# The end of a state-space layer: output projections of the last two groups, summed in one accumulation or apart

## The chip, the cores and the metric

One core of a Trainium2 chip runs the whole program in one launch. The metric is the device time of one execution in microseconds, as the median of three runs. The engines are TensorE (PE, with its weight loads listed as PEld), VectorE (DVE), ScalarE (ACT), GpSimd (POOL) and SyncE (SP), which issues nearly all DMAs.

## The reference, cut to what matters

The model is a trunk of two layers of three sub-layers each: an FFN, a mixer, an FFN, every one with a scaled residual and a layer norm behind it. The mixer of the first layer is a bidirectional Mamba-2 (state-space) block, that of the second a differential attention. The change touches the end of the state-space block. There are 512 positions, 1024 model channels, and an inner width of 2048 in four groups of 512.

```python
y = y_f + y_b + X * d_skip.astype(f32)[:, None]
y = y.reshape(b, t, D_INNER) * jax.nn.silu(z.astype(f32))
yg = y.reshape(b, t, SSM_GROUPS, D_INNER // SSM_GROUPS)
yg = yg * lax.rsqrt(jnp.mean(jnp.square(yg), axis=-1, keepdims=True) + LN_EPS)
y = yg.reshape(b, t, D_INNER) * norm_g.astype(f32)
return y.astype(u.dtype) @ w_out
...
x = layer_norm(ALPHA * x + gate(1) * y, ln_g[i, 1], ln_b[i, 1])
y = swiglu(modulate(x, mods[:, 2]), ffn_w_gate[i, 1], ffn_w_up[i, 1], ffn_w_down[i, 1])
```

Each group has its own RMS norm (the "gated norm"), so the output projection of a group can start when that group's scan and norm are done. The four groups' contributions to `y @ w_out` are summed.

## The kernel before, in words

Activations are kept transposed: channels on the 128 partitions, positions along the free dimension. The residual `x` is eight blocks of 128 channels by 512 positions (`res[0]` to `res[7]`). Every float32 operand of a projection is split into a high and a low part (`split` for weights, lines 107 to 125, one pass of ScalarE and one of DVE; `split_act` for activations), and a product is three matmuls: high by high, high by low, low by high (`mm3`, line 172). All projections are recorded at line 176. One output block of one group has four blocks of 128 in its inner dimension, hence 12 matmuls over 512 positions, or twice 12 over 256 positions where it is done in halves. The sum goes into a PSUM tile (`acc`; 4 banks of that tag, 2 of "mid", 2 of "ln"). `add_res` (line 400, recorded at L401) multiplies it by the gate and adds it to the residual on DVE.

`ssm` (line 651) works group by group. A scan of a group has eight steps (four pairs of heads by two halves of the sequence). Each step makes decay matrices: a DMA of broadcast rows (`rw`, `ch`), masks on POOL (L840), exponentials on ScalarE (L848 to L851), a sum on POOL (L854), a product with `cb` on DVE (L855), and then 12 matmuls on PE (L865). Between the steps the code puts "units" of other work, from a list `todo`: convolution projections of the next group, the `z` projections of this group, and output projections (`outp`, two output blocks a call, 24 matmuls) of the group before. After the projections of a group come its SiLUs in one batch (L775, with a change of ScalarE's function table before and after), and `prepare` builds the next group's matrices. Before the change the units of a scan are these, in written order:

- group 1: ten projections, then the four output units of group 0
- group 2: ten projections, then the four output units of group 1
- group 3: four `z` projections, then two of the four output units of group 2; the other two stand behind the last gated norm

`gated_norm` (line 867) multiplies by SiLU(z) (L870), sums squares (L872 to L876), makes four columns of statistics with matmuls (L879), takes the power -1/2 on POOL (L258), and in `rest` broadcasts the result with transposes (L264) and normalizes (L888, L153, L154). For groups 0 to 2 it is issued inside the scan of the next group; for group 3 nothing of a scan is left.

The layer norm behind the block subtracts a provisional mean first, the mean over the first residual block's channels (`LN.shift`, line 293: a copy at L297, a matmul at L298, a copy at L300, and four subtractions over pairs of blocks at L303). Before the change it is issued with the first output unit of group 2.

The last group's output runs through `down_units` (line 418) with KEEP 6: blocks 0 and 1 over all positions, blocks 2 to 7 kept for `finish` (line 436), which does them first for positions 0 to 255, then for 256 to 511. After each block `feed` updates the sums for the norm (L311 to L317). After each half come the statistics (`stats`: L323, L327, L332 to L341, L345) and a generator that normalizes this half (`normalize`: L368, L373, L375) while the next half's blocks are multiplied. The next FFN's first products work on the first half while the second is still being normalized; its first block over all positions stands in a "mid" bank. Beside it runs `ada_stream`, which computes the next layer's modulation from weights (DMA `in_adaw`, DVE L195).

The attention layer ends in another way, with `merged_units` (line 456). It takes two sets of four inner blocks, `old` (ready early) and `new` (ready late). Output blocks 0 to 3 are done for `old` and for `new` apart. For blocks 4 to 7 the products of both sets go into one accumulation of 24 matmuls per half; of blocks 4 and 5 the `old` products of the first half are begun early, in the "mid" banks. It is a generator: each `next` issues one block, so the caller can put blocks between other steps, and `shut` and `gated` (lines 164 to 170) tell the planner to order a matmul of the norm behind the last projection issued so far.

The code is written for a tile framework: it allocates buffers from pools with a fixed number of slots, sets all semaphores, and plans the order of each engine's instructions from its own model of time, with the written order as the priority. So the order run can differ from the order written. The pool `ap` has 32 tiles of 128 by 512 (`big`): inputs, states, normalized groups and the first weights of the next FFN live there. Weights arrive in four `raw` tiles and are split into a ring of three (`wp`). The tiles of the scan (`ep`: `rw`, `ch`, `dx`, `E` with five slots) are open until the end of the layer.

Of the kernel before, what the change touches and what calls it, by code (L numbers as in the profile page):

```python
# [14 lines left out]
P = 128  # L15
# [7 lines left out]
NG = 4  # L23
# [23 lines left out]
def hybrid_trunk(tc, xT, cb, par, cst, adaw, wgu, wdn0, wdn1, wdn2, wdt, win, wso, wqk, wv, wao, dist_in, dtp, lam_in, out):  # L47
    nc = tc.nc
# [13 lines left out]
    def big(dt=F32, name="big"):  # L62
        return ap.tile([P, T], dt, tag="a", name=name)
# [4 lines left out]
    def acc(tag="acc"):  # L68
        return ps.tile([P, T], F32, tag=tag, name=tag, bufs=BANKS[tag])
# [10 lines left out]
    invg = cp.tile([P, 1], F32, name="invg")  # L80
# [81 lines left out]
    last_mm, gate = [None], [None]  # L162

    def gated(x):
        if gate[0] is not None:
            tc.add_manual_dep(x.ins, gate[0].ins.name, NOSYNC, reason="behind a projection")
        return x

    def shut():
        gate[0] = last_mm[0]  # L170
# [11 lines left out]
    def proj(o, w, u, m=P, cols=FULL, prev=None):  # L182
        for a, b in cols:
            prev = mm3(
                o[:m, a:b], [(w[k][0], w[k][1], u[k][0][:, a:b], u[k][1][:, a:b]) for k in range(len(u))], prev
            )
        last_mm[0] = prev
        return prev
# [59 lines left out]
    def advance(g, n):  # L248
        for _ in range(n):
            if g is None or next(g, "end") == "end":  # L250
                return
# [148 lines left out]
    def add_res(d, pd, n, a, b):  # L400
        nc.vector.scalar_tensor_tensor(  # L401
            out=res[d][:, a:b], in0=pd[:, a:b], scalar=gvec[n][:, d : d + 1], in1=res[d][:, a:b],
            op0=ALU.mult, op1=ALU.add,
        )
# [13 lines left out]
    def down_units(n, u, units, ln=None, KEEP=4):  # L418

        last = ln is not None  # L420
        keep = []
        for ld in units:
            for d, w in ld():
                if last and d >= KT - KEEP:
                    keep.append((d, w))
                    continue
                pd = acc()
                proj(pd, w, u)
                add_res(d, pd, n, 0, T)
                if last:  # L430
                    ln.feed(d, 0, T)
            yield
        if last:
            finish(n, ln, [(d, w, u) for d, w in keep])
# [18 lines left out]
        next_u[0] = ln.u  # L453
        ln.residual()

    def merged_units(n, ln, old, wo, wn, home):

        half = len(old)
        for q in range(2):
            w = split(load(wo[q]))  # L460
            for e in range(2):
                pd, d = acc(), 2 * q + e
                proj(pd, w[e * 4 : e * 4 + 4], old)
                add_res(d, pd, n, 0, T)
                if d == 0:
                    shifting = ln.shift()
                advance(shifting, 1)
                yield
        w0 = {2: split(load(wo[2]), home=home[0])}
        begun = {}  # L470
        for e in range(2):
            pd = acc("mid")
            proj(pd, w0[2][e * 4 : e * 4 + 4], old, cols=HALVES[:1])
            begun[4 + e] = (pd, half)
            yield
        new = yield
        for q in range(2):
            w = split(load(wn[q]))
            for e in range(2):
                pd, d = acc(), 2 * q + e  # L480
                proj(pd, w[e * 4 : e * 4 + 4], new)
                add_res(d, pd, n, 0, T)
                ln.feed(d, 0, T)
        keep = []
        for q in range(2, 4):
            w1 = split(load(wn[q]), home=home[q - 1])
            if q == 3:
                w0[3] = split(load(wo[3]), home=home[3])
            for e in range(2):
                c = slice(e * 4, e * 4 + 4)  # L490
                keep.append((2 * q + e, w0[q][c] + w1[c], old + new))
        finish(n, ln, keep, begun)

    def send(g, x):
        try:
            g.send(x)
        except StopIteration:
            pass
# [140 lines left out]
    def wide_units(w):  # L639
        def mk(q):  # L640
            def ld():
                s = split(load(w[q]))
                return [(q * 2 + e, s[e * 4 : e * 4 + 4]) for e in range(2)]
            return ld
        return [mk(q) for q in range(4)]
# [5 lines left out]
    def ssm(n):  # L651
        u = next_u[0]
        sc = ExitStack()
        ep = sc.enter_context(tc.tile_pool(name="ep", bufs=2))
        dp = sc.enter_context(tc.tile_pool(name="dp", bufs=1, space=bass.MemoryType.DRAM))
        masks = big(name="masks")
        nc.sync.dma_start(masks, cst[:, 2 * P :])
# [206 lines left out]
                    rhs = mats[hh][:, k * W : (k + 1) * W] if k < 2 else chs[hh][:, cc]  # L864
                    nc.tensor.matmul(py[hh * 64 : (hh + 1) * 64, cc], lhsT=lhs, rhs=rhs, start=k == 0, stop=k == 2)  # L865

        def gated_norm(g, ys, zs):
            ss = big(name="gss")
            for k in range(4):
                nc.vector.tensor_tensor(out=ys[k], in0=ys[k], in1=zs[k], op=ALU.mult)  # L870
                if k == 0:
                    nc.scalar.activation(ss, ys[k], AF.Square)  # L872
                else:
                    sq = tmp("sq")
                    nc.scalar.activation(sq, ys[k], AF.Square)
                    nc.vector.tensor_tensor(out=ss, in0=ss, in1=sq, op=ALU.add)  # L876
            st = acc("ln")
            for i in range(4):
                nc.tensor.matmul(st[:, i : i + 1], lhsT=ss[:, i * P : (i + 1) * P], rhs=invg, start=True, stop=True)  # L879
            r = rstd(st[:, :4], 4)  # L880

            def rest():
                rb = acc("ln")
                bcast_cols(rb, r[:, :4])
                yr = []
                for k in range(4):
                    o = tmp("yn")
                    nc.vector.scalar_tensor_tensor(  # L888
                        out=o, in0=ys[k], scalar=pc(C_NG + g * 4 + k), in1=rb, op0=ALU.mult, op1=ALU.mult
                    )  # L890
                    yr.append(split_act(o))
                return yr

            return rest

        def run(units):
            for f in units:
                f()
# [3 lines left out]
        bc, xs, zs = [], [], [[] for _ in range(NG)]  # L902
# [6 lines left out]
        run(units_z(0, zs[0])[:2])  # L909
        cur = prepare(0, xs, bc)  # L910
        outs, yrs = {}, {}
        ln, shifting = LN(n), []
        norm = None

        def outp(gg):
            if gg not in outs:
                outs[gg] = down_units(n, yrs[gg], wide_units(wso[gg]))
                if gg == NG - 2:
                    shifting.append(ln.shift())
            next(outs[gg])  # L920
            if shifting:
                advance(shifting[0], 2)

        for g in range(NG):
            xt, cbs, states, Ct = cur
            nbc, nxs = [], []
            first = units_z(g, zs[g])[len(zs[g]) :]
            if g < NG - 1:
                first = units_bc(g + 1, nbc) + units_x(g + 1, nxs) + first
            todo = first + ([lambda gg=g - 1: outp(gg)] * 4 if g > 0 else [])  # L930
            tot, done, batched = len(todo), 0, False
            for s in range(8):
                pr_, c = divmod(s, 2)
                ft = g * 4 + pr_
                if c == 0:
                    heads = [ssd_head(ft * 2 + hh, Ct) for hh in range(2)]
                    py = acc("mid")
                mats = [ssd_mats(ft * 2 + hh, c, heads[hh][0], heads[hh][2], cbs) for hh in range(2)]
                ssd_out(pr_, c, py, mats, [hd[1] for hd in heads], xt, states)
                if c == 1:  # L940
                    nc.vector.scalar_tensor_tensor(
                        out=xs[pr_], in0=xs[pr_], scalar=pc(C_D + ft), in1=py, op0=ALU.mult, op1=ALU.add
                    )
                if s == 0 and norm is not None:
                    rest = norm()
                if s == 2 and norm is not None:
                    yrs[g - 1] = rest()
                while done < tot - (2 if g == NG - 1 else 0) and done < (s + 1) * tot // 8:
                    todo[done]()
                    done += 1  # L950
                if done >= len(first) and not batched and (s >= 6 or done == tot):
                    batched = True
                    silu(zs[g] + nbc + nxs)
                    if g < NG - 1:
                        cur = prepare(g + 1, nxs, nbc)
            norm = (lambda g=g, xs=xs: gated_norm(g, xs, zs[g]))
            xs = nxs
        yr = norm()()
        run(todo[done:])
        advance(shifting[0], 4)  # L960
        for _ in down_units(n, yr, wide_units(wso[NG - 1]), ln, 6):
            pass
        sc.close()


# [306 lines left out]
```

## Time and profile before

| | us |
|---|---|
| median of three runs | 2182.35 (2177.52 to 2185.12) |
| the profiled execution | 2177.95 |
| its span, first to last instruction | 2176.1 |
| PE busy | 2120.5 (97%) |
| DVE busy | 1765.4 (81%) |
| ACT busy | 1092.2 (50%) |
| POOL busy | 155.2 (7%) |

The scans take about 460 to 776 us of the span, with group 3's first matmul at 720.9 us; the last gated norm, the last output blocks and the layer norm go to about 840 us. The attention layer's end lies between about 1756 and 1834 us.

How to read the views: a wait row gives the engine that waited, who released it, then the total in us, the times and the longest. A chain row gives start, us and what ran, merged over neighbours with their count. A timeline row gives start, us, engine, line, operation, operands, count and, in brackets, the idle time before it and its releaser. Window rows give the stretch, its length, busy time of each engine with the count of its instructions, the granted share of TensorE's clock, the DMA share and GB/s. A busy PE is not PE at its peak, so the text counts matmuls and their spacing. A few per cent of the matmul records may be missing.

### The profile page before, as it was taken

The page shows a single profiled execution, that of the slowest core. Times are in us where ns is not written, and L with a number is a line of the kernel's source. Part 1 is how long each engine was busy: PE and PEld are TensorE (multiplying, and loading weights), DVE is VectorE, ACT ScalarE, POOL GpSimd, SP SyncE. Part 2 cuts the span into 40 slices and gives each one's busy share as a digit, 9 for nine tenths or more (in the row PEclk, how much of TensorE's full clock was granted, in tenths as well). Part 3 has the DMA queues.
Part 4 walks back from the last instruction along what each step waited for, and adds up shares of the span by engine and source line. Part 5 has one row for each costly group of instructions (what it writes and reads, how often), then busy time and mean ns, then how long its engine had stood idle before and what let it go on. Part 6 is the DMA issues. An engine that isn't in the chain of part 4 may idle for free.

```text
span 2176.1 us, 34041 instructions
## 1 busy us (share of the span) xinstructions
PE 2120.5 (97%) x13206; PEld 1857.6 (85%) x13206; DVE 1765.4 (81%) x2934; ACT 1092.2 (50%) x1828; POOL 155.2 (7%) x258
## 2 busy tenths in 40 slices
PE   7999999999999998999999999999999999999997
PEld 6889899866777677989899989899988878989897
DVE  6979998556666688979988998997777888958696
ACT  4424354757656546434355534344766647524353
POOL 0000000034332310000000000000111100000000
PEclk9999999999999998999999999999999999999999
DMA  8853644464445413554533272733322212423231
GB/s 320 304 213 118 222 130 166 115 181 136 145 126 158 123 64 126 174 185 153 196 125 112 95 265 92 254 100 124 89 78 78 88 44 84 136 70 116 77 117 40
DMA packets 90082, 301.19 MB, mean 138 GB/s; under 512 B 10048, under 2 KB 13504, under 8 KB 89920
## 3 DMA queue, kind: packets, MB, share of 16 engines
q1 hardware_dynamic: 88384, 294.81, 41.3%
q0 software_dynamic: 1536, 4.20, 0.9%
q8 instruction: 104, 1.70, 0.3%
q14 instruction: 58, 0.48, 0.1%
HBM read 289.53 MB, written 5.24 MB: 135 GB/s over the span
## 4 chain that ended last, share of the span: by engine, by line
PE 84%; DVE 5%; issue 4%; ACT 3%; POOL 2%; DMA 2%; POOLq 0%; SPq 0%; ACTq 0%; DVEq 0%
PE acc L176 67%; PE mid L176 10%; PE mid L865 2%; DMA raw<-in_adaw 1%; PE mid L1033 1%; DVE raw L195 1%; POOL E L854 1%; PE ln L176 1%; PE ln L813 1%; DMA raw<-in_wdn 0%; ACT wh L123 0%; ACT p L1043 0%; PE ln L1055 0%; POOL dx L840 0%; PE ln L264 0%
## 5 line engine op out<-in xcount | busy, mean ns | idle before, releaser
L176 PE MATMUL acc<-hi,wh 128*128 128x256 f32 (+1 forms) x1576 | 526.9, 336 | 3.1 <-ACT hi L153 1.9
L176 PE MATMUL acc<-hi,wl 128*128 128x256 f32 (+1 forms) x1576 | 525.9, 334 | 0.0
L176 PE MATMUL acc<-lo,wh 128*128 128x256 f32 (+1 forms) x1576 | 525.6, 334 | 0.3 <-DVE lo L154 0.2
L176 PE MATMUL acc<-uh,wh 128*128 128x256 f32 (+1 forms) x1160 | 391.8, 338 | 0.2 <-ACT wh L123 0.2
L176 PE MATMUL acc<-ul,wh 128*128 128x256 f32 (+1 forms) x1160 | 390.5, 337 | 0.0
L176 PE MATMUL acc<-uh,wl 128*128 128x256 f32 (+1 forms) x1160 | 389.5, 336 | 0.0
L123 ACT ACTIVATE wh<-raw 128x1024 fp32r<-128x1024 f32 (+1 forms) x210 | 213.0, 1022 | 272.7 <-DMA raw<-in_wdn 95.9
L528 ACT ACTIVATE wh<-raw 128x1024 fp32r<-128x1024 f32 x198 | 209.1, 1059 | 254.1 <-DVE raw L538 121.8
L176 PEld LDWEIGHTS acc<-hi,wh 128*128 128x128 f32 x1576 | 297.9, 189 | 40.1 <-ACT hi L153 5.2
L176 PEld LDWEIGHTS acc<-lo,wh 128*128 128x128 f32 x1576 | 298.0, 189 | 31.8 <-DVE lo L154 1.9
L176 PEld LDWEIGHTS acc<-hi,wl 128*128 128x128 f32 x1576 | 298.0, 189 | 29.9 <-issue 0.5
L124 DVE TENSOR_TENSOR wl<-raw,wh 128x1024 fp32r<-128x1024 f32 (+1 forms) x210 | 248.0, 1184 | 47.6 <-ACT wh L123 46.7
L529 DVE TENSOR_TENSOR wl<-raw,wh 128x1024 fp32r<-128x1024 f32 x198 | 241.2, 1220 | 24.0 <-ACT wh L528 23.0
L176 PEld LDWEIGHTS acc<-uh,wh 128*128 128x128 f32 x1160 | 219.3, 189 | 29.6 <-issue 6.6
L176 PEld LDWEIGHTS acc<-ul,wh 128*128 128x128 f32 x1160 | 219.7, 189 | 24.9 <-issue 3.3
L176 PEld LDWEIGHTS acc<-uh,wl 128*128 128x128 f32 x1160 | 219.7, 189 | 23.9 <-issue 2.4
L538 DVE TENSOR_TENSOR raw<-raw 128x512 f32<-128x512 f32 x264 | 181.3, 689 | 4.7
L195 DVE SCALAR_TENSOR_TENSOR raw<-raw,cond 128x1024 f32<-128x1024 f32 x144 | 174.1, 1221 | 9.6 <-DMA raw<-in_adaw 9.4
L401 DVE SCALAR_TENSOR_TENSOR resid<-acc,gv,resid 128x512 f32<-128x512 f32 (+1 forms) x164 | 108.6, 667 | 71.1 <-PE acc L176 70.8
L341 POOL TENSOR_TENSOR rr<-vr,mhalf 128x2 f32<-128x2 f32 x12 | 9.5, 789 | 1512.9 <-DVE vr L337 1512.9
L176 PE MATMUL mid<-uh,wh 128*128 128x256 f32 (+2 forms) x332 | 99.6, 302 | 0.6 <-DVE up L570 0.6
L176 PE MATMUL mid<-uh,wl 128*128 128x256 f32 (+2 forms) x332 | 99.3, 299 | 0.0
(267 smaller groups left out, 3939.6 us busy)
## 6 DMA issues: line engine op xcount, KB each, us to landing
raw<-in_wgu SPq DMA_DIRECT2D x176, 512.0 KB, 4.0
raw<-in_adaw SPq DMA_DIRECT2D x144, 512.0 KB, 4.7
raw<-in_wdn SPq DMA_DIRECT2D x64, 448.0 KB, 4.0
raw<-in_win SPq DMA_DIRECT2D x40, 512.0 KB, 3.8
raw<-in_wdn SPq DMA_DIRECT2D x32, 512.0 KB, 4.7
rw<-scr SPq DMA_DIRECT2D x32, 512.0 KB, 5.5
ch<-scr SPq DMA_DIRECT2D x32, 256.0 KB, 3.6
raw<-in_wso SPq DMA_DIRECT2D x16, 512.0 KB, 3.6
```

Of the source, the lines that this page charges most:

```text
L123: nc.scalar.activation(hi[:, :n], raw, AF.Copy)
L124: nc.vector.tensor_tensor(out=lo[:, :n], in0=raw, in1=hi[:, :n].bitcast(F32), op=ALU.subtract)
L176: last = nc.tensor.matmul(o, lhsT=a, rhs=b, start=start and j == 0, stop=j == n - 1, skip_group_check=not start)
L195: nc.vector.scalar_tensor_tensor(out=raw, in0=raw, scalar=1.0, in1=cond, op0=ALU.mult, op1=ALU.mult, accum_out=mods[l][:, j : j + 1],)
L401: nc.vector.scalar_tensor_tensor(out=res[d][:, a:b], in0=pd[:, a:b], scalar=gvec[n][:, d : d + 1], in1=res[d][:, a:b], op0=ALU.mult, op1=A ...
L528: nc.scalar.activation(x[0], r, AF.Copy)
L529: nc.vector.tensor_tensor(out=x[1], in0=r, in1=x[0].bitcast(F32), op=ALU.subtract)
L538: nc.vector.tensor_tensor(out=o, in0=x, in1=y, op=ALU.add)
L813: nc.tensor.matmul(pst, lhsT=bt[:, i * P : (i + 1) * P], rhs=xd, start=o == 0, stop=o == 1)
L854: nc.gpsimd.tensor_tensor(out=dg, in0=dg, in1=dx[:, c], op=ALU.add)
L865: nc.tensor.matmul(py[hh * 64 : (hh + 1) * 64, cc], lhsT=lhs, rhs=rhs, start=k == 0, stop=k == 2)
L1033: nc.tensor.matmul(ss[m], lhsT=q[:, c], rhs=qks[h, 1][m], start=j == 0, stop=j == 1)
```

## The change

The last two groups' outputs go through `merged_units`, with group 2's normalized blocks as `old` and group 3's as `new`:

- Output units move by two: of group 1's four, two stay at the end of group 2's scan and two go to the end of group 3's. None of group 2's stand inside a scan.
- The last gated norm gets a `fill`: two output blocks of group 2 are issued ahead of its statistics, and one between the power and the broadcast. The matmuls of the norm are ordered behind them. Block 3 and the begun halves of blocks 4 and 5 follow after the broadcast.
- Output blocks 4 to 7 sum groups 2 and 3 in one accumulation, in halves; blocks 0 to 3 of group 3 go over all positions.
- `shift` is created before the scans and advanced one step at a time in group 3's scan, from step 3 on.
- The pool `ep` is closed after the scans, and a weight ring `wy` of three is opened in its place for three of the late weight tiles.

For the attention layer `merged_units` does the same as before.

```diff
-    def merged_units(n, ln, old, wo, wn, home):
+    def merged_units(n, ln, old, wo, wn, home, shifting=None):
...
-                if d == 0:
-                    shifting = ln.shift()
+                shifting = shifting or ln.shift()
                 advance(shifting, 1)
...
-        def gated_norm(g, ys, zs):
+        def gated_norm(g, ys, zs, fill=None):
...
+            if fill:
+                fill(2)
             st = acc("ln")
             for i in range(4):
-                nc.tensor.matmul(st[:, i : i + 1], lhsT=ss[:, i * P : (i + 1) * P], rhs=invg, start=True, stop=True)
+                gated(nc.tensor.matmul(st[:, i : i + 1], lhsT=ss[:, i * P : (i + 1) * P], rhs=invg, start=True, stop=True))
...
             def rest():
+                if fill:
+                    fill(1)
                 rb = acc("ln")
...
-        ln, shifting = LN(n), []
+        ln = LN(n)
+        shifting = ln.shift()
...
-            todo = first + ([lambda gg=g - 1: outp(gg)] * 4 if g > 0 else [])
+            late = lambda gg, k: [lambda: outp(gg)] * k
+            todo = first + (late(0, 4) if g == 1 else late(1, 2) if g > 1 else [])
...
-                while done < tot - (2 if g == NG - 1 else 0) and done < (s + 1) * tot // 8:
+                while done < (s + 1) * tot // 8:
...
+                if g == NG - 1 and s > 2:
+                    advance(shifting, 1)
...
-        yr = norm()()
-        run(todo[done:])
-        advance(shifting[0], 4)
-        for _ in down_units(n, yr, wide_units(wso[NG - 1]), ln, 6):
-            pass
+        es.close()
+        wy = sc.enter_context(tc.tile_pool(name="wy", bufs=3))
+        tail = merged_units(n, ln, yrs[NG - 2], wso[NG - 2], wso[NG - 1], (wy, wy, None, wy), shifting)
+
+        def fill(k):
+            for _ in range(k):
+                next(tail)
+            shut()
+
+        yr = norm(fill)()
+        gate[0] = None
+        for _ in range(4):
+            next(tail)
+        send(tail, yr)
```

More of the change, by code (lines that the diff above doesn't have):

```diff
@@ L653, in ssm @@
         sc = ExitStack()
-        ep = sc.enter_context(tc.tile_pool(name="ep", bufs=2))
+        es = ExitStack()
+        ep = es.enter_context(tc.tile_pool(name="ep", bufs=2))
         dp = sc.enter_context(tc.tile_pool(name="dp", bufs=1, space=bass.MemoryType.DRAM))
@@ L917, in outp @@
                 outs[gg] = down_units(n, yrs[gg], wide_units(wso[gg]))
-                if gg == NG - 2:
-                    shifting.append(ln.shift())
             next(outs[gg])
-            if shifting:
-                advance(shifting[0], 2)
         for g in range(NG):
@@ L955, in ssm @@
                         cur = prepare(g + 1, nxs, nbc)
-            norm = (lambda g=g, xs=xs: gated_norm(g, xs, zs[g]))
+            norm = (lambda fill=None, g=g, xs=xs: gated_norm(g, xs, zs[g], fill))
             xs = nxs
-        yr = norm()()
-        run(todo[done:])
-        advance(shifting[0], 4)
-        for _ in down_units(n, yr, wide_units(wso[NG - 1]), ln, 6):
-            pass
+        es.close()
[10 more added lines that the diff above has]
+        send(tail, yr)
         sc.close()
```

## The prediction

> **What bounds the kernel now.** I read the page first, then PE's waits around the end of the state-space layer, then windows and the chain there, and last the same views of the attention end, which already runs the `merged_units` tail.
>
> ```profile
> span 2176.1 us, 34041 instructions
> PE 84%; DVE 5%; issue 4%; ACT 3%; POOL 2%; DMA 2%; POOLq 0%; SPq 0%; ACTq 0%; DVEq 0%
> ```
>
> TensorE carries 84% of the chain that ended last, so time is won where PE waits or runs slowly. The sum of products is the same before and after; hence I count losses of PE only. From the scan of group 3 to the first block after the norm, PE waits three times:
>
> ```profile
> PE ln L298 <- ACT z L297: 1.9, 1, 1.9
> PE ln L264 <- POOL rr L258: 1.2, 1, 1.2
> PE mid L865 <- DVE ch L826: 0.7, 1, 0.7
> ```
>
> From the LN statistics of the first half to the first full-width block of the next FFN (columns: total us, times, longest):
>
> ```profile
> PE acc L176 <- DVE ul L375: 4.2, 4, 1.3
> PE ln L264 <- POOL rr L341: 3.0, 2, 2.7
> PE acc L176 <- DVE wal L116: 1.1, 2, 0.7
> ```
>
> The same stretch at the attention end:
>
> ```profile
> PE acc L176 <- DVE ul L375: 1.1, 1, 1.1
> PE ln L264 <- POOL rr L341: 0.9, 1, 0.9
> PE mid L323 <- DVE sc L316: 0.4, 1, 0.4
> PE acc L176 <- DVE resid L401: 0.2, 1, 0.2
> ```
>
> Waiting is 8.3 us in one and 2.6 us in the other. The clock adds to it. In these windows of the projections' line L176 the columns are us, PE busy (matmuls), weight loads, granted clock, DMA share, GB/s:
>
> ```profile
> 762.60:765.80 3.20, 2.37 (x6) 1.89 (x7) 0.50 0.29 86
> 817.20:830.70 13.50, 6.96 (x26) 5.94 (x26) 0.50 0.11 39
> 1800.60:1834.40 33.80, 29.07 (x228) 27.82 (x229) 1.00 0.28 94
> 805.10:851.70 46.60, 34.71 (x247) 32.50 (x247) 0.85 0.32 107
> ```
>
> After the wait for `z` and in the LN tail PE was granted half its clock, for 3.2 and 13.5 us; in the attention tail the clock stayed whole.
>
> **The change part by part.** Time of one matmul first, from undisturbed pieces of the chain (start, us, times):
>
> ```profile
> 715.97 5.04 PE acc L176 x22
> 1823.63 11.00 PE acc L176 x92
> ```
>
> 512 columns take 5.04 / 22 = 0.229 us, 256 columns 11.00 / 92 = 0.1196 us. A unit of two output blocks (24 matmuls) is 5.5 us.
>
> *A, the tail.* Before, six blocks of group 3 run in halves with 12 matmuls each; after, four blocks with 24. The work of DVE per block stays the same, so PE has more to do for each thing DVE does. Stretches that end at the same point of the program, the first full-width block of the next FFN, compare: 46.60 us with 247 matmuls, 46.60 - 247 x 0.1196 = 17.1 us beside them; 33.80 us with 228, 6.5 us beside them. The difference, 10.6 us, is what this stretch would gain if the end behaved as attention's does. The cause is visible on DVE in the stretch from the first statistics to 822.2 us:
>
> ```profile
> L401 DVE SCALAR_TENSOR_TENSOR resid<-acc,gv,resid 128x256 f32<-128x256 f32 x6 | 2.8, 482 | 0.0
> L317 DVE TENSOR_TENSOR ss<-ss,sq 128x256 f32<-128x256 f32 x6 | 2.5, 421 | 0.0
> L316 DVE TENSOR_TENSOR sc<-sc,resid 128x256 f32<-128x256 f32 x6 | 2.5, 421 | 0.0
> ```
>
> Six blocks cost DVE 7.8 us while it also normalizes the first half; with four it is 5.2 us, 2.6 us less, and meanwhile PE has up to 96 x 0.1196 = 11.5 us of second-half products instead of 72 x 0.1196 = 8.6 us. One thing here is not in the attention end: the adaLN stream of the next FFN stands on DVE between the last `ul` steps, behind a DMA.
>
> ```profile
> 832.84 4.51 DMA raw<-in_adaw
> 836.41 0.39 PE L176 MATMUL acc<-ul,wah 128*128 128x256 f32 x1 [0.83 <-DVE ul L375]
> 839.34 0.39 PE L176 MATMUL acc<-ul,wah 128*128 128x256 f32 x1 [0.87 <-DVE ul L375]
> ```
>
> I leave those 0.83 + 0.87 = 1.7 us in place: A = -(10.6 - 1.7) = -8.9 us. Bounds: -10.6 (nothing stays), and -2.6 (DVE's own saving alone, the clock still halved). I take the value near the attention rows because tail, shapes and next step are the same code there.
>
> *B, the provisional mean.* Before, `shift()` copies block 0 after the first output block of group 2, and the copy stands on ScalarE behind the batch of SiLUs:
>
> ```profile
> 757.59 1.28 ACT L775
> 758.89 1.67 ACT z L775 x3
> 761.13 0.50 PE L298 MATMUL ln<-z,onesn 128*128 128x512 f32 x1 [1.93 <-ACT z L297]
> ```
>
> After, it stands at scan step 3 and reads a block that group 1's output unit finished at the end of group 2's scan; the SiLUs are written behind it, at step 6. It issues no DMA. The 1.93 us go, and with them the half-rate stretch, worth at most 3.2 / 2 = 1.6 us. I keep 0.4 us for the copy's turn: B = -(1.9 + 1.6 - 0.4) = -3.1; bounds -3.5 and 0. Four subtractions over pairs (L303, one per step) still go to DVE; the step's `E` and `ch` products queue behind them, and PE waits for those; that price is in E.
>
> The Trainium skill, page "TensorE: Matmul & The Clock Gate", Part 1, says that the clock falls to half after at least one idle window of about 3.4 us. The trace does not agree: a wait of 1.93 us came before the first stretch. By the page no stretch would follow such waits, before or after; the sum goes by the trace.
>
> *C, the last gated norm.* Behind it in order, with what covers its steps now:
>
> ```profile
> 776.57 5.91 PE acc L176 x25
> 782.49 0.80 PE ln L879 x8
> 783.55 1.95 POOL rr L258
> 786.20 19.12 PE acc L176 x127
> 788.21 0.69 DVE L154 TENSOR_TENSOR lo<-yn,hi 128x512 fp32r<-128x512 f32 x1
> ```
>
> The added order: the statistics (L879) stand in PE's queue behind two blocks, 5.5 us in place of 5.9; the broadcast (L264) behind a third, 2.7 us, for a chain over DVE and POOL that took 786.20 - 0.65 - 782.49 = 3.1 us; then one block and two half blocks, 2.7 + 2.9 = 5.6 us, before the first products of group 3, for a chain of 788.21 + 0.69 - 785.55 = 3.4 us. PE is left with some 0.8 us where it waited 1.2: C = -0.4. Bounds: 0 wait (-1.2), and, if the planner spends these blocks earlier, all three chains bare: at most 5.9 + 3.1 + 3.4 = 12.4 us. I take the first, as 19 us of projections (an output unit of group 1 and the old halves) are written behind the last scan step.
>
> *D, widths.* 24 matmuls of 512 become 48 of 256: 24 x (2 x 0.1196 - 0.229) = +0.2 us. The longer accumulation adds no matmul. Four adds of 512 and four of 256 columns leave DVE; they count in A only.
>
> *E, less cover in the scan.* Group 2's scan loses two units, 11.0 us. The place is from its SiLU batch to the first scan step of group 3:
>
> ```profile
> 687.40:720.90 33.50, 24.26 (x96) 1.00 0.38 110
> 720.90:776.40 55.50, 38.13 (x152) 0.97 0.37 109
> PE ln L813 <- DVE xd L809: 1.1, 1, 1.1
> ```
>
> There 96 matmuls (four units) cover the SiLUs and `prepare`, after the change 48; PE already waits 1.1 us for `xd`. In group 3 the count is nearly unchanged: 152 before, 144 written after, with the old halves ready to move up. That projections do move up, out of written order, shows where pieces of the scan alternate with an output unit:
>
> ```profile
> 770.33 1.44 PE mid L865 x10
> 771.77 1.13 PE acc L176 x4
> 775.13 1.44 PE mid L865 x10
> ```
>
> The other bound is group 0, which has eight units for its eight steps:
>
> ```profile
> 459.50:502.70 43.20, 38.15 (x174) 0.92 0.68 182
> PE mid L865 <- DVE E L855: 4.9, 2, 4.5
> ```
>
> 43.20 - 38.15 = 5.05 us idle, and 0.08 x 43.2 = 3.5 us for the clock: 8.5 us. I take +2.0, nearer to group 2, whose ending this is; ends -0.7 (the `ch` wait goes) and 8.5.
>
> At nothing: the loads (16 of `in_wso` before and after, on SP in the order of use; the old half of the last wide unit comes last and has the first half's products as cover, 8.6 us), and the new weight ring, which lies where the scan's tiles were and is first written after the last scan step. One shortage: group 1's products now live to step 7, so at step 5 the tiles of size 512 in use come to 33 of 32 (xs 4, zs 4, C 1, xt 4, cb 2, states 2, two sets of normalized y 16); the last `z` copy waits until step 6 frees two. One unit, 5.5 us, covers it; without cover it costs the same step again, inside E.
>
> Sum: -8.9 - 3.1 - 0.4 + 0.2 + 2.0 = -10.2 us. The profiled execution took 2177.95 us, 1.85 us around its span, 4.4 us under the median of 2182.35: 2177.95 becomes 2167.8, the median 2172.2.
>
> **Rivals.** *The tail keeps its waits* (chance 0.10): A is worth only DVE's 2.6 us, as the adaLN stream and the weight splits fill what four blocks leave free. -2.6 - 3.1 - 0.4 + 0.2 + 2.0 = -3.9: 2178.5. For it: L195's steps and their DMA in the chain. Against: of the 8.3 us of waits only the 1.7 stand behind that DMA.
>
> *Half clock again* (0.06): a wait as short as B's was enough for it, and C or the first `ul` may leave one. A stretch of 13.5 us costs up to 6.7: -10.2 + 6.7 = -3.5, 2178.9. Against: attention's tail has waits of 1.1 and 0.9 us and a clock of 1.00. The page named above speaks for none here, as no wait comes near 3.4 us.
>
> *The scan runs bare* (0.15, the slower side): at the end of group 2 nothing moves up, so PE idles for the missing 11.0 us, and group 3 then runs like group 0, 8.5 us. 19.5 in place of E's 2.0: -12.2 + 19.5 = +7.3, 2189.7. It decides once PE loses over 12.2 us more than now between 687 us and the end of the scan. For it: the chain there runs through POOL, ScalarE and the DMA of `rw`, not PE alone; against: the alternation above.
>
> *It does not do what it says* (0.03): the planner orders the products as before; no change, 2182.
>
> **How the numbers follow.** The forecast has 0.66. Its own ends: A -10.6, B -3.5, C -1.2, D, E 0 give -15.1, 2167; with the spread of the runs, 2177.5 to 2185.1, 2163; at the upper end E at 5 gives 2175. The range goes up to 2184 to take in three rivals and leaves out the bare scan. A measurement of this kernel tells 0.3%, 6.5 us, from no change: faster is the forecast, 0.66; same the first two rivals and the last, 0.19; slower 0.15.
>
> **What would show it.** Right: no wait of L298 on `z`; granted clock 1.00 from the scan to the FFN; the stretch from the first L323 to the first full-width block near 36 to 38 us; no long wait before group 3's first scan step. Wrong: PE waits for `E`, `xd` or `st` of several us around that step; a half-rate stretch after it; `ul` waits still at 4 us.

## The result and the profile after

| | before | after |
|---|---|---|
| median, beside each other | 2179.93 us (4 runs, 2176.78 to 2185.12) | 2161.29 us (4 runs, 2158.99 to 2163.03) |
| ratio, 95% interval | | 0.9915 [0.99, 0.9931] |
| again, on a chip of the experiments | 2176.86 us (15 runs) | 2161.24 us (6 runs) |
| ratio, 95% interval | | 0.9923 [0.9908, 0.9937] |
| profiled execution | 2177.95 us | 2160.72 us |

The change gains 15.6 us by the larger set, where 10.2 were forecast, and its median lies below the range's lower end of 2163. The page of the kernel after begins like this (span, then the chain's shares by engine):

```profile
span 2158.9 us, 34079 instructions
...
PE 82%; DVE 7%; issue 4%; ACT 3%; DMA 2%; POOL 2%; POOLq 0%; SPq 0%; ACTq 0%; DVEq 0%
```

The waits of PE from the end of group 2's scan to the next FFN, in total us, times, longest:

```profile
PE ln L813 <- DVE xd L809: 2.2, 3, 1.3
PE acc L176 <- DVE wal L116: 1.0, 1, 1.0
PE mid L865 <- DVE E L855: 0.7, 1, 0.7
PE acc L176 <- ACT uh L373: 0.6, 1, 0.6
PE mid L865 <- DVE ch L826: 0.2, 1, 0.2
```

The waits for `z` (L298), for `rr` (L258 and L341) and for `ul` are gone. One is larger, for `xd`, at the place of the fewer covering units. The provisional mean's matmul now follows the product before it without a gap (timeline of PE):

```profile
732.08 0.39 PE L176 MATMUL acc<-uh,wl 128*128 128x512 f32 x1
732.30 0.40 PE L298 MATMUL ln<-z,onesn 128*128 128x512 f32 x1
```

And the windows of line L176 (us, PE busy and matmuls, weight loads, granted clock, DMA share, GB/s), first the scan, then the end from the first L323 to the first full-width block:

```profile
716.00:762.00 46.00, 34.77 (x147) 26.98 (x146) 1.00 0.44 124
793.70:832.10 38.40, 34.15 (x274) 33.07 (x274) 1.00 0.25 84
```

The end took 46.6 us with 247 matmuls at a clock of 0.85 and takes 38.4 with 274 at 1.00.

To place the gain, I went through PE's records in order and summed, for each matmul, the time until the next one starts beyond its undisturbed spacing: 0.2275 us for 512 columns, 0.114 for 256, 0.0605 for 128, 0.06 for one. That is PE's **loss**: waits, half clock and short gaps together, whatever the order of the products. Four stages: S1 from group 2's first scan matmul to the statistics of its gated norm, S2 to the statistics of group 3's, S3 to the first L323, S4 to 865 us. The first cuts are points of the program; 865 us is a time, by which a faster kernel has done more of the next FFN, with its short gaps.

| kernel | S1 | S2 | S3 | S4 | sum | median less that of before on the same chip, us | ratio, 95% interval |
|---|---|---|---|---|---|---|---|
| before | 15.1 | 13.4 | 2.7 | 17.2 | 48.4 | | |
| after | 17.3 | 8.3 | 1.8 | 6.8 | 34.2 | -18.6 | 0.9915 [0.99, 0.9931] |
| after_again | 17.4 | 8.4 | 1.7 | 8.1 | 35.6 | -15.6 | 0.9923 [0.9908, 0.9937] |
| b_four | 15.1 | 12.3 | 4.1 | 12.5 | 44.0 | -5.5 | 0.9978 [0.9966, 0.9989] |
| b_eight | 15.1 | 13.6 | 4.3 | 16.5 | 49.5 | 0.0 | 0.9998 [0.9989, 1.0007] |
| b_mean_early | 15.1 | 10.7 | 4.4 | 9.7 | 39.9 | -9.7 | 0.9954 [0.9941, 0.9966] |
| b_early_w | 15.2 | 13.5 | 5.7 | 7.1 | 41.5 | -7.7 | 0.9967 [0.9954, 0.9979] |
| b_both | 15.3 | 11.3 | 5.6 | 7.1 | 39.3 | -9.7 | 0.9958 [0.9945, 0.997] |
| b_three | 15.2 | 11.1 | 6.0 | 9.8 | 42.1 | -5.8 | 0.9971 [0.9959, 0.9983] |
| a_apart | 17.3 | 8.3 | 1.6 | 6.3 | 33.5 | -15.7 | 0.9925 [0.9912, 0.9939] |
| a_late_w | 17.5 | 8.6 | 1.5 | 9.1 | 36.7 | -13.5 | 0.9935 [0.9922, 0.9949] |
| a_mean_tail | 17.2 | 8.7 | 1.6 | 7.0 | 34.5 | -12.6 | 0.9941 [0.9928, 0.9953] |
| a_nofill | 17.4 | 9.5 | 5.0 | 5.9 | 37.8 | -11.5 | 0.9948 [0.9936, 0.9961] |
| a_units4 | 15.3 | 9.8 | 2.8 | 8.1 | 36.0 | -12.6 | 0.9944 [0.9931, 0.9958] |
| a_early_w | 17.3 | 8.3 | 4.0 | 5.6 | 35.2 | -14.7 | 0.9933 [0.9921, 0.9946] |
| a_early_both | 17.3 | 7.8 | 3.4 | 5.8 | 34.3 | -9.2 | 0.996 [0.9948, 0.9973] |

Names with b_ start from the kernel before, with a_ from the one after. The last run lost its time elsewhere (below). For the other experiments the sum of one profiled execution, set against before's 48.4, agrees with the medians within 1.8 us; for the change itself it says 14.2 and 12.8, where the medians say 18.6 (before's own median stood 3.1 us higher there) and 15.6; the difference is not placed. (after_again's 8.1 in S4 holds a half-rate stretch of 3.4 us that the first execution lacks.) So the gain lies in these stages: S1 +2.2, S2 -5.1, S3 -0.9, S4 -10.4, sum -14.2 us. The loss ahead of S1 was 3.7 us larger before than after, at code that the change does not touch; over the sixteen traces it lies anywhere from 62.9 to 69.4 us, so that is no gain of the change. For the end of the layer the prediction's own sum can be done again up to the first full-width block: 46.60 - 247 x 0.1196 = 17.1 us before, 38.40 - 274 x 0.1196 = 5.6 us after, 11.5 us less.

### The profile page after: what moved, and what is told of

Same layout as the page of the kernel before. It is cut to its first block, busy times and chain, and to the rows that moved or that the text cites. A ratio compares the mean times of both kernels' runs of the same rounds, so it can differ in the third digit from the quotient of the medians.

```text
span 2158.9 us, 34079 instructions
## 1 busy us (share of the span) xinstructions
PE 2113.4 (98%) x13230; PEld 1854.8 (86%) x13230; DVE 1761.3 (82%) x2924; ACT 1088.2 (50%) x1824; POOL 159.5 (7%) x258
## 3 DMA queue, kind: packets, MB, share of 16 engines
q1 hardware_dynamic: 88384, 294.81, 42.1%
## 4 chain that ended last, share of the span: by engine, by line
PE 82%; DVE 7%; issue 4%; ACT 3%; DMA 2%; POOL 2%; POOLq 0%; SPq 0%; ACTq 0%; DVEq 0%
PE acc L176 66%; PE mid L176 10%; PE mid L865 2%; PE ln L176 1%; PE mid L1046 1%; DMA raw<-in_wdn 1%; DVE wl L124 1%; POOL E L854 1%; DVE raw L195 1%; DMA raw<-in_wgu 1%; ACT wh L123 1%; ACT p L1056 0%; PE ln L813 0%; PE ln L1068 0%; DVE wal L116 0%
## 5 line engine op out<-in xcount | busy, mean ns | idle before, releaser
L176 PE MATMUL acc<-hi,wh 128*128 128x256 f32 (+1 forms) x1568 | 522.5, 335 | 2.8 <-ACT hi L153 1.7
L176 PE MATMUL acc<-hi,wl 128*128 128x256 f32 (+1 forms) x1568 | 522.8, 334 | 0.0
L176 PE MATMUL acc<-lo,wh 128*128 128x256 f32 (+1 forms) x1568 | 521.8, 333 | 0.3 <-DVE lo L154 0.2
L176 PE MATMUL acc<-uh,wh 128*128 128x256 f32 (+1 forms) x1160 | 391.5, 338 | 0.0
L176 PE MATMUL acc<-ul,wh 128*128 128x256 f32 (+1 forms) x1160 | 390.4, 337 | 0.0
L176 PE MATMUL acc<-uh,wl 128*128 128x256 f32 (+1 forms) x1160 | 389.2, 336 | 0.0
L176 PEld LDWEIGHTS acc<-hi,wh 128*128 128x128 f32 x1568 | 295.9, 189 | 37.5 <-ACT hi L153 4.7
L176 PEld LDWEIGHTS acc<-lo,wh 128*128 128x128 f32 x1568 | 296.1, 189 | 30.8 <-DVE lo L154 2.3
L176 PEld LDWEIGHTS acc<-hi,wl 128*128 128x128 f32 x1568 | 296.1, 189 | 29.5 <-issue 0.5
L176 PEld LDWEIGHTS acc<-uh,wh 128*128 128x128 f32 x1160 | 219.1, 189 | 29.8 <-issue 7.4
L176 PEld LDWEIGHTS acc<-ul,wh 128*128 128x128 f32 x1160 | 219.4, 189 | 25.3 <-issue 3.9
L176 PEld LDWEIGHTS acc<-uh,wl 128*128 128x128 f32 x1160 | 219.4, 189 | 24.3 <-issue 3.0
L195 DVE SCALAR_TENSOR_TENSOR raw<-raw,cond 128x1024 f32<-128x1024 f32 x144 | 173.9, 1219 | 10.7 <-DMA raw<-in_adaw 10.6
L341 POOL TENSOR_TENSOR rr<-vr,mhalf 128x2 f32<-128x2 f32 x12 | 9.2, 766 | 1515.5 <-DVE vr L337 1515.5
L176 PE MATMUL mid<-uh,wh 128*128 128x256 f32 (+2 forms) x332 | 99.8, 302 | 0.7 <-DVE up L569 0.7
L176 PE MATMUL mid<-uh,wl 128*128 128x256 f32 (+2 forms) x332 | 99.3, 299 | 0.0
```

The lines of the kernel that those rows point to most:

```text
L176: last = nc.tensor.matmul(o, lhsT=a, rhs=b, start=start and j == 0, stop=j == n - 1, skip_group_check=not start)
L195: nc.vector.scalar_tensor_tensor(out=raw, in0=raw, scalar=1.0, in1=cond, op0=ALU.mult, op1=ALU.mult, accum_out=mods[l][:, j : j + 1],)
L341: nc.gpsimd.tensor_tensor(out=r[:, :m], in0=vr[:, :m], in1=mhalf[:, :m], op=ALU.pow)
```

## The experiments

**Blocks in halves, without the rest of the change.** The forecast put A on DVE's adds for six halved blocks and on the products that PE has at hand. Two runs change only the count of halved blocks:

```
-        for _ in down_units(n, yr, wide_units(wso[NG - 1]), ln, 6):
+        for _ in down_units(n, yr, wide_units(wso[NG - 1]), ln, 4):
```

(b_eight has 8 there, and a weight ring of three more buffers.)

> The kernel before, with four blocks of group 3 done in halves instead of six; nothing is accumulated across groups. Theory 'balance' (PE loses in the tail what DVE's work during the second half exceeds PE's products there): before 7.8 + 7.2 us of DVE against 8.6 us of PE, an excess of 6.4 us; here 5.2 + 7.2 against 5.7, 6.7 us: +0.3 us against the kernel before. Theory 'fewer adds' (DVE's smaller work is the gain): -2.6 us. Theory 'more products' (PE's cover alone): +2.9 us.

> The kernel before, with all eight blocks of group 3 done in halves (a second weight ring in the place of the scan's tiles holds their weights). Theory 'balance': DVE 10.4 + 7.2 us against 11.5 us of PE products in the second half, an excess of 6.1 us, so -0.3 us against the kernel before. Theory 'fewer adds': +2.6 us. Theory 'more products': -2.9 us.

Four blocks gained 4.8 to 5.5 us and eight changed nothing. No theory has both: fewer adds would have made eight blocks slower, more products would have made four slower.

**Apart instead of in one sum.** From the kernel after; each of six half blocks now sums the two groups in two banks with its own add:

```
+                    if begun and n == 1:
+                        proj(pd, w[:4], u[:4], cols=((a, b),))
+                        add_res(d, pd, n, a, b)
+                        pd = acc()
+                        w, u = w[4:], u[4:]
```

> The changed kernel, but six of the eight half blocks 4 to 7 of the state-space end are summed apart: the old group's 12 matmuls with an add of their own, then the new group's 12. PE's work is the same; DVE has six more adds of 256 columns, four of them in the second half (some 1.6 us). Theory 'balance': the excess of DVE grows from 0.9 to 2.5 us, +1.6 us against the changed kernel and still some 14 us under the kernel before. Theory 'fewer adds': +2.9 us against the changed kernel for six adds of 0.48. Theory 'more products': no change.

No change against after (2160.24 and 2161.24 us), with six more adds. The accumulation that the change is named after is worth nothing by itself, and DVE's adds do not set the tail. What it carries is the order: products of group 2 stay at hand for the end.

**The mean alone.** Into the kernel before:

```
-        ln, shifting = LN(n), []
+        ln = LN(n)
+        shifting = ln.shift()
...
+                if g == NG - 1 and s > 2:
+                    advance(shifting, 1)
```

> The kernel before, with only the provisional mean moved: created ahead of the scans, one step from scan step 3 of group 3 on. The prediction's term B says -3.1 us (the wait for z of 1.9 us and half of a half-rate stretch of 3.4 us, less 0.4). The rival: the SiLU batch and its changes of table hold ScalarE at that place anyway, PE meets the same wait at the next decay matrices, and it gains under 1 us.

It gained 9.7 us, three times B. The stages show that only 2.7 are in the scan (S2); 7.5 are in the tail (S4), where this run has no edit, and 1.7 are given back in S3. The scan's 2.7 hide more: now that the scan ends earlier, PE waits there for the sum of squares `gss` of the last gated norm, where the kernel before never waited.

```profile
PE ln L879 <- DVE gss L876: 2.1, 1, 2.1
```

Without that wait S2 would be 8.6 us, near the 8.3 of the kernel after. The kernel before, in the tail, on PE:

```profile
815.75 0.39 PE L176 MATMUL acc<-ul,wah 128*128 128x256 f32 x1 [1.28 <-DVE ul L375]
817.97 0.58 PE L176 MATMUL acc<-ul,wah 128*128 128x256 f32 x1 [1.24 <-DVE ul L375]
819.24 0.58 PE L176 MATMUL acc<-uh,wal 128*128 128x256 f32 x1 [0.69 <-DVE wal L116]
827.25 0.69 PE L264 MATMUL ln<-csts,rr 128*128 128x128 f32 x2 [2.74 <-POOL rr L341]
```

`wal` is the low half of the next FFN's first weights: three blocks of weights, each in two halves, so six splits at L116. While the first half is normalized, pairs of `ul` come one by one, and PE can multiply each pair only with weights that are split. How many were there up to 808 us is one row of line L116 (durations min, median, max in ns, first and last start); the kernel before, then the one with the mean moved:

```profile
L116 DVE TENSOR_TENSOR wal<-raw,wah x1: 689/689/689, 800.9 to 800.9; 128x512 fp32r<-128x512 f32 x1
```

```profile
L116 DVE TENSOR_TENSOR wal<-raw,wah x3: 679/681/685, 787.0 to 797.4; 128x512 fp32r<-128x512 f32 x3
```

The same row has three for b_four, one for b_eight, four for the kernel after. That gave a new theory, of the weights: the tail's loss follows how many are split in time.

**The weights alone.** From the kernel before; the three blocks are written ahead of the last output units:

```
         run(todo[done:])
         advance(shifting[0], 4)
+        ahead.append(first_units(2))
...
-    ffn(2, st1, (1, 2, 0), first7=4)
+    ffn(2, st1, (1, 2, 0), ahead[0], first7=4)
```

> The kernel before, with one line moved: the first weights of the next FFN (three blocks, six halves) are loaded and split ahead of the last group's output units instead of behind the whole layer in written order; all else as before. Theory of the weights (formed on the traces of the runs so far): what PE loses in the LN tail follows how many of the six halves are split when the products of the layer itself run out. PE's loss beyond the nominal time of its matmuls from 790 to 860 us was 17.7 us before (one half split by then), 12.7 with four blocks in halves (three), 10.0 with the mean moved (three), 6.7 after the change (four). It expects 5 to 8 us less than before, 2168 to 2171 us on this chip's 2176, and a loss of 10 to 12 us in the tail. Theory of the prediction (the adds of the halved blocks on DVE are the cause; they stay): between -1 and +1 us.

7.7 us less, at the top of what that theory expected; six splits were there, and S4 fell from 17.2 to 7.1:

```profile
L116 DVE TENSOR_TENSOR wal<-raw,wah x6: 682/684/685, 787.4 to 795.1; 128x512 fp32r<-128x512 f32 x6
```

What it gave back is in S3 (+3.0): in the waits of PE from 777 to 865 us the layer's own weights now stand behind the new splits on DVE.

```profile
PE acc L176 <- DVE ul L375: 1.8, 2, 1.1
PE acc L176 <- DVE wl L124: 1.2, 1, 1.2
PE mid L323 <- DVE sc L316: 1.0, 1, 1.0
```

**The reverse, from the kernel after.** Five of the six splits ordered behind the first half's last sum of squares (`behind` is in the code already; `first_half` holds that square and that sum, and `n_free` lets one half pass):

```
+    behind[:], n_free[0] = first_half, 1
+    pre2 = first_units(2)
+    behind.clear()
-    ffn(2, st1, (1, 2, 0), first7=4)
+    ffn(2, st1, (1, 2, 0), pre2, first7=4)
```

> The kernel after, with five of the six halves of the next FFN's first weights ordered, on ScalarE and on DVE, behind the last sum of squares of the first half (in the kernel after, four were split 14 us before that); nothing else changed. Theory of the weights: the tail loses again what it lost before, 6 to 10 us more than after, 2167 to 2171 us. Theory of the prediction (fewer adds and longer products in the tail, both still there): no change, -1 to +1.5 us.

Only two were split by 808 us, yet its median is 1.7 us above after_again's, not 6 to 10. The six executions of after_again lie between 2156.67 and 2163.09 us, so a difference of 1 or 2 us among the runs from the kernel after is hardly clear of noise.

```profile
L116 DVE TENSOR_TENSOR wal<-raw,wah x2: 683/688/694, 777.6 to 796.6; 128x512 fp32r<-128x512 f32 x2
```

The theory of the weights alone falls. The reading that is left is that PE needs *something* to multiply while half a norm is computed, the next FFN's products or its own. Windows of L176 over 16 us, from about 1 us behind the first L323, show what the kernel before lacked and the one after has; first before, then after:

```profile
806.00:822.00 16.00, 10.62 (x72) 9.54 (x73) 0.85 0.09 34
```

```profile
795.00:811.00 16.00, 14.78 (x120) 14.48 (x121) 1.00 0.24 86
```

**Is one cover enough?** The weights early in the kernel after (the same line, ahead of `send`), and both small moves together in the kernel before:

> The kernel after, with the first weights of the next FFN written ahead of the last group's products, as the run on the kernel before had it (there 7.7 us less). Theory of cover: the tail needs products at hand while half a norm is computed, its own longer halves or the next FFN's, and one of them is enough; the merged tail has the first: -1 to +1 us. Theory of the weights alone (the earlier, the better): 3 to 6 us less than after, as six halves are split in place of four.

> The kernel before with two moves of earlier runs together: the provisional mean ahead of the SiLU batch (alone: 9.7 us less) and the next FFN's first weights ahead of the last output units (alone: 7.7 us less). Output units and tail as before, nothing merged. Theory 1, shared: of the early mean's 9.7 us, 7.7 were in the tail, where it only let the weights be split earlier; then the two gain the tail once, 10 to 12 us less than before. Theory 2, the mean's subtractions on DVE are a cause of their own: 15 to 18 us less, as much as the whole change.

a_early_w: 0.7 us above after_again's median, though all six were split. b_both: -9.7, as the mean alone. The mean's 7.5 us and the weights' 10.1 in S4 were one gain taken twice. No run takes both covers from the kernel after, so that either one is enough there is seen from each side alone (a_late_w and a_early_w). With the third cheap move, four blocks in halves:

```
-        for _ in down_units(n, yr, wide_units(wso[NG - 1]), ln, 6):
+        for _ in down_units(n, yr, wide_units(wso[NG - 1]), ln, 4):
```

> The kernel before with three moves and nothing merged: mean early, the next FFN's weights early, and four blocks in halves in place of six. Theory of cover: the tail's loss falls from the 9.7 us of the run with two moves to 6 or 7, the scan keeps its own: 12 to 14 us less than before in all; what is left to the kernel after, 2 to 4 us, are the last gated norm's waits (2.8 us for the sum of squares in the run with two moves), which only old blocks ordered between its steps cover. Rival: the merged halves themselves are needed, and it stays at 9 to 10 us less.

A miss for both: -5.8 us, by the medians 3.9 us worse than without that move, though the two intervals overlap. Waits from 765 to 830 us:

```profile
PE ln L880 <- DVE gss L877: 2.8, 1, 2.8
PE acc L176 <- DVE wl L124: 1.7, 1, 1.7
```

Two more full-width blocks run ahead of the halves and want their weights while DVE splits the next FFN's; and ahead of group 3's statistics nothing is left to cover the sum of squares `gss`. Both are what old blocks of group 2, kept for the end, cover in the kernel after. I take this from the waits; no run removes just these two. The wait for `gss` is as long in b_both, so it is not what made this run slower than that one. The clock is a better candidate: from 770 to 825 us b_three ran 10.2 us at half rate and b_both 3.4, and half of the difference, 3.4 us, is about what it lost; why it has the longer stretches was not tested.

**The order inside the last gated norm.** From the kernel after:

```
-        yr = norm(fill)()
-        gate[0] = None
-        for _ in range(4):
+        yr = norm()()
+        for _ in range(7):
```

> The kernel after, with the last gated norm written in one piece ahead of all seven old blocks of the tail, as before the change, without the ordering that holds its matmuls behind projections. Term C of the prediction: +0.4 us (up to +1.2), as the planner moves projections up by itself. The rival bound, that without the written order the three chains of the norm lie bare: +5 to +12 us.

3.7 us above after_again's median, between the two: S2 +1.1, S3 +3.3 against after_again. Its waits from 740 to 800 us:

```profile
PE ln L881 <- DVE gss L876: 1.4, 1, 1.4
PE mid L865 <- DVE E L855: 0.4, 1, 0.4
PE ln L264 <- POOL rr L258: 0.4, 1, 0.4
```

A half-rate stretch of 6.8 us follows at 759.3 us. The written order with its gates is worth this; without it the planner left the waits above.

**The mean in the tail** (`shift` where the attention layer has it), and **the units back in group 2's scan**:

```
-        tail = merged_units(n, ln, yrs[NG - 2], wso[NG - 2], wso[NG - 1], (wy, wy, None, wy), shifting)
+        tail = merged_units(n, ln, yrs[NG - 2], wso[NG - 2], wso[NG - 1], (wy, wy, None, wy))
```

```
-            todo = first + (late(0, 4) if g == 1 else late(1, 2) if g > 1 else [])
+            todo = first + (late(g - 1, 4) if g in (1, 2) else [])
```

> The kernel after, with the provisional mean put back into the tail: taken after the first output block of the merged tail, as the attention layer does, and its four subtractions one per block behind it. Term B of the prediction: +3.1 us (0 to +3.5). If what the early mean gained alone in the kernel before (9.7 us) is its own: +9 to +10. Theory of the weights: the mean's own part is the wait of PE in the scan, which does not come back here since the copy stands behind no SiLUs; DVE has 4.6 us more to do ahead of the splits, so +1 to +4.

> The kernel after, with all four output units of group 1 in group 2's scan again and none in group 3's. Term E of the prediction (two units less cover at group 2's end cost 2.0 us; the trace after shows 1.8 us more loss from 620 to 700 us): 1 to 2.5 us less than after, if the old blocks of the tail move up into group 3's scan by themselves. Rival: they don't, and PE lies bare in group 3's scan, 5 to 11 us more than after.

a_mean_tail is 2.6 us above after_again's median, but its four stages lose what after's do (34.5 and 34.2, 35.6), so I can't say that the mean's place makes this difference; as far as the stages show, what matters is that it leaves the place behind the SiLUs. a_units4 is 2.9 us above: S1 falls from 17.3 to 15.3, which is term E taken back, and S2 to S4 give back 3.8 against after (2.5 against after_again, which has the same half-rate step in S4). That this comes from the two units that group 3's scan and the last norm have less is argued, not shown.

**The attention layer's weights too** (the line of a_early_w once more, for the FFN behind attention):

> The run before this one, and the same for the attention layer: its next FFN's first weights written ahead of the last four heads' products. The attention end waits 2.6 us and lost some 1.7 us to half clock in one stretch. Theory of cover: it has merged products too, so -1 to +1 us against the run before. Theory of the weights: 2 to 4 us less than the run before.

5.5 us above a_early_w. The wait for `ul` there is gone, and a larger one has come, for attention's own output weights:

```profile
PE acc L176 <- ACT wh L123: 7.2, 1, 7.2
```

SP's queue shows why: two of the next FFN's loads went ahead of that of `in_wao`. A stretch of 10.2 us at half clock begins in that wait, at 1771.8 us.

```profile
1766.54 2.85 SPq L99 DMA_DIRECT2D raw<-in_wgu  x2
1771.46 0.33 SPq L99 DMA_DIRECT2D raw<-in_wao  x1
```

**The kernel after again**, as the base for the runs above:

> The kernel after, unchanged, beside the other run on the same chip, as the base for the runs that take one part from it. From the run that sums six halves apart and the result: 15 to 17 us less than before on this chip, 2159 to 2162 us.

2161.24 us, as expected. None of these versions is clearly faster than the kernel after; a_apart's median is 1.0 us lower, within the spread of the runs.

## Why the prediction was right or wrong

The direction, the mechanism (less loss of PE, not less work) and the place were right: the wait of L298 gone, the clock 1.00 from the scan to the FFN (after_again has one half-rate step of 3.4 us at 815 us), the end 38.4 us where 36 to 38 were named. None of the rivals came at its price. What failed are two sizes in the sum, A and B, and the base that the sum was put on: the gain was larger than forecast, and the time that it was taken from was lower.

- **A, -8.9; measured -10.4 (S4; -9.1 in after_again), -11.5 by its own sum.** Near the bound of -10.6, the attention end as model. The step that failed is "I leave those 0.83 + 0.87 = 1.7 us in place": no wait for `ul` is left. Of the two causes given, more products at hand is the one that the runs bear out; DVE's saved adds fall with a_apart. What was not seen is the second cover, the next FFN's weights: the prediction saw `wal` among the waits (1.1 us) and did not ask how many were split.
- **B, -3.1, with -3.5 as its bound; measured -5.1 (S2).** This is the term with the largest error. Moved alone, the mean gave 2.7 in S2, but with a new wait of 2.1 us for `gss` in it; without that wait it is 13.4 - 8.6 = 4.8. The wait of 1.9 us and half of a 3.4 us step are 3.6 of it; the 0.4 us kept "for the copy's turn" were not needed, and the other 1.2, in shorter waits and gaps, had no term. The whole move alone is worth 9.7 us, but 7.5 of them are the tail's, which A already counts.
- **C, -0.4; S3 -0.9.** Against the kernel before that was the right order. But the last scan ends earlier after B, and then the sum of squares is late (2.1 us with the mean moved alone, 1.4 in a_nofill, no wait in the kernel after): without the written order the new kernel would lose 3.7 us. The prediction set the new order against the waits of the kernel before; a wait that only appears once another is removed was not priced.
- **D, +0.2**: too small to be seen in any run.
- **E, +2.0; measured +2.2 (S1)**, and a_units4 takes it away to 0.2. PE waits 2.2 us for `xd` in place of 1.1, at the row that the prediction had named.
- **The base.** -10.2 was put on 2182.35, the median of three runs, and the 4.4 us between the profiled execution and that median were carried along. Fifteen runs give 2176.86 us, below the profiled execution, and the 9 to 19 runs of before beside each of the other experiments 2175.98 to 2176.67. So, with 2176.86 as the base, 5.5 us of the 10.9 by which 2172.2 misses 2161.3 are the base and 5.4 the effect; the range around 2176.9, shifted by the same 5.5 us, would have been 2157.5 to 2178.5. (Its lower end, by its own working, is 2177.5 - 15.1 = 2162.4 and not 2163; the measured 2161.3 lies below both.)

## What to carry to other kernels

Where PE waits at the seam of two layers, list what it could multiply there and whether each product's weights are loaded and split by then; here one cover was enough, and two edits that supplied the same cover did not add up. When one wait goes, price the next one in line on the same chain. And moving the next layer's weights forward helps only as far as their loads and splits don't stand ahead of this layer's own.

## What the runs showed of the hardware

The clock fell to half for 3.41 us or a multiple of it, on a grid of the same step that ran through each execution. Counted over all sixteen traces, from 100 us on, with the modelled ends of the matmuls: of 77 such steps in which PE was idle for half or more, 75 were followed by half clock; of 92 with 30 to 50% idle, 34; of 9495 with less, 17. One such step in the kernel before, with the wait for `z` in it, and the step after it (us, PE busy and matmuls, granted clock, DMA share, GB/s):

```profile
759.10:762.50 3.40, 1.47 (x12) 1.00 0.00 0
762.50:765.90 3.40, 3.40 (x12) 0.50 0.27 82
```

So a wait of 1.9 us costs its length once, and up to 1.7 us more (half of 3.41) where it falls within one step: the wait for `z` of 1.9 us was followed by half clock in before, b_early_w and b_eight, and not in b_four, where it lay across two steps and PE was idle for 48% of the first. The Trainium skill, page "TensorE: Matmul & The Clock Gate", Part 1, says that the window runs freely, and the traces agree: the same code met half clock at 414 us in some executions and not in others. Its rule, an idle window, is too strict by these counts: a step that is idle for half does it too.
